# Last stage of a two-layer trunk: where the weight sums for four of eleven pairs of blocks are made

## The chip, the cores and the metric

The kernel runs on one core of a Trainium2 chip. The metric is device microseconds of one execution; the kernel before took 1689.75 us as the median of three runs (1689.26, 1689.75 and 1690.2). The engines are named as the profile names them: PE (matrix multiply; PEld is its weight load), DVE (vector), ACT (scalar), POOL (GpSimd) and SP, which only issues DMAs here. POOL and ACT issue DMAs too. Each engine takes its instructions in one fixed order and waits at the first one whose inputs or buffers are not ready.

## The reference, cut to what matters

Two residual layers, 512 positions, width 1024. Each layer has a token mixer with three branches, an output projection, and a gated feed-forward block with a causal convolution; a last RMSNorm follows. The change touches how the second layer's down projection gets its weights:

```python
def conv_ffn(h, w_up, conv_w, conv_b, w_down):
    u = h @ w_up                                  # 512 x 1024 by 1024 x 5632
    ...
    gate, val = jnp.split(c, 2, axis=-1)          # 2 x 2816 columns
    return (jax.nn.silu(gate) * val) @ w_down     # 2816 x 1024
...
    x = x + conv_ffn(rmsnorm(x, norm2_g[l]), ffn_w_up[l], ffn_conv_w[l], ffn_conv_b[l], ffn_w_down[l])
return rmsnorm(x, final_g)
```

## The kernel before, in words

**Numbers.** Every fp32 product is made of three matmuls on parts: a value is split into hi (a rounded copy, made by ACT) and lo (the rest, made by DVE as value minus hi), and `mm3` (line 153) multiplies hi by lo, hi by hi and lo by hi. A weight block of 128 x 512 is a *unit*: `load` (line 122) fetches it over SP's queue into a raw buffer, `part` (line 131) splits it (ACT copy at line 140, DVE subtraction at line 141), and the matmuls at line 157 use it. `unit` (line 95) works ahead by a plan of all units known beforehand: for the last stage's units (pool "q") it splits up to 4 units ahead of the one in use (`AHEAD`) and loads up to 6 ahead of the splits (`DEEP`). Hi and lo of three units in five go to ring buffers of three (tiles wh and wl), of the other two to the general pool of 31 tiles, tag "u" (tiles sh and sl).

**The order of the program.** First layer: mixer, output projection, up projection `ffn_up` (22 steps), down projection `ffn_down` (line 1160, 8 steps). Second layer: mixer, output projection, `ffn_up`, and then `last` (line 1182), the second down projection with the final norm.

**The last stage.** The 2816 rows of the second layer's w_down are 22 blocks of 128; block pair q (0 to 10) has blocks 2q and 2q+1, each cut into two halves of 512 columns: four quarters, b[0] to b[3]. `last` multiplies by a scheme with seven products per pair in place of eight. Four of them, p = 7, 5, 6, 4, need sums of the quarters: 7 is b3 - b1, 5 is b1 - b0, 6 is b0 plus sum 7, and 4 is b2 minus sum 6. **The first phase** of `last` runs through the pairs with these four products (44 units, n = 4q for p = 7, then 5, 6, 4); each unit feeds six matmuls. The PSUM tiles of products 7 and 5 are named acc in the profile, those of 6 and 4 are named sm. Later phases use the plain quarters.

**Where the sums were made before.** `presum` (line 246) makes them ahead of time in the first layer: on a call it finishes the pair that is pending (four DVE sums at lines 251 to 254 and four stores to DRAM from POOL's queue at line 257, tiles ts) and starts the next one by the table `PRE` (four loads from POOL's queue at line 262, tiles pre). Pairs 0 to 3 are started in steps 2, 4, 6, 8 of the first `ffn_up`, pairs 4 to 10 one after each of the first seven steps of the first `ffn_down`. The first phase of `last` then loads the finished sums over SP's queue (wr<-ts) and splits them.

**Beside the splits** the first phase makes others: `side(n)` (line 1206) fetches stored activations over SP's queue, and splits one (`both`, lines 1200 to 1204: an ACT copy at 1202 and a DVE subtraction at 1203) after every fourth unit and another after every eighth. From pair 2 on (`self.keep = q > 1`) splits and these others stay in program order on their engines: copy and subtraction of unit n + 4, then those of `side(n)`, then those of unit n + 5.

At the start of the first phase DVE and ACT also finish the last step of `ffn_up`: the convolution (lines 1125 to 1132) and `halves` (lines 1144 to 1158), which takes one of the three wh buffers.

Of the kernel before, what the change touches and what calls it, by code (L numbers as in the profile page):

```python
# [13 lines left out]
ADD, SUB, MUL, POW, MAX = ALU.add, ALU.subtract, ALU.mult, ALU.pow, ALU.max  # L14
# [9 lines left out]
FIRST = (12, 4, 0, 8)  # L24
FILL = (36, 2, 1)
KEPT = 6
PRE = {(0, "f", 2): 0, (0, "f", 4): 1, (0, "f", 6): 2, (0, "f", 8): 3, (0, "d", 0): 4, (0, "d", 1): 5, (0, "d", 2): 6, (0, "d", 3): 7,
       (0, "d", 4): 8, (0, "d", 5): 9, (0, "d", 6): 10}
SEQ = "0 H G G 0 S 0 U U G G 0 S 0 0 S 2 2 Y 0 0 2 1 2 1 2 1 2 1 2 1 2 1 1 1"
NRAW = 3  # L30
AHEAD = {None: 2, "p": 4, "r": 3, "f": 3, "u": 5, "q": 4}
# [21 lines left out]
class Emit:  # L53
# [67 lines left out]

    def load(self, u, queue=None):
        name, l, i, c0, n, _ = u
        raw = self.u(n="wr") if u[5] in ("q", "u") and self.nraw % 2 else self.wp.tile([128, 512], F32, name=self.nm("wr"), tag="wr", bufs=NRAW)
        src = self.tsum[i] if name == "tsum" else self.a[name][l, i]
        with self.tc.high_priority():
            self.kept((queue or self.nc.sync).dma_start(raw[:, :n], src[:, c0:c0 + n]))
        self.raws.append(raw)
        self.nraw += 1

    def part(self, u):
        raw, n, pool = self.raws.pop(0), u[4], u[5]

        self.turn = (self.turn + 1) % 5 if pool in ("p", "q") else 4
        if pool is None or self.turn < 3:
            hi, lo = [self.wp.tile([128, 512], F32R, name=self.nm(t), tag=t, bufs=3) for t in ("wh", "wl")]
        else:
            hi, lo = [{"f": self.f, "r": self.r, "u": self.u, "p": self.u, "q": self.u}[pool](dt=F32R, n=t) for t in ("sh", "sl")]
        with self.tc.high_priority() if pool in (None, "p", "q") else nullcontext():
            self.kept(self.nc.scalar.copy(hi[:, :n], raw[:, :n]))  # L140
            self.kept(self.nc.vector.tensor_tensor(lo[:, :n], raw[:, :n], hi[:, :n], op=SUB))  # L141
        self.parts.append((hi, lo))
        self.npart += 1
# [102 lines left out]
    def presum(self, l, stage, m):  # L246

        if self.pre:
# [6 lines left out]
            for p, t in zip((7, 5, 6, 4), (b[3], b[1], b[0], b[2])):  # L255
                self.tsum[q, p] = self.dp.tile([128, 512], F32, name=self.nm("ts"))
                self.nc.gpsimd.dma_start(self.tsum[q, p], t)
        q = PRE.get((l, stage, m))
        if q is not None:
# [89 lines left out]
    def run(self):  # L349
        nc, tc, a, V = self.nc, self.tc, self.a, self.nc.vector  # L350
        self.con = self.cp.tile([128, NCC], F32, name="con")
        self.pre, self.tsum = [], {}
        self.rst = self.cp.tile([128, 512], F32, name="rst")
        self.bonesR = self.cp.tile([128, 128], F32R, name="bonesR")
        self.ones = self.cp.tile([128, 128], F32R, name="ones")
        V.memset(self.rst, 1.0)
        wu = self.acc()
        for i in range(5):
            nc.tensor.matmul(wu[:, 0:256], self.rst[:, 0:128], self.rst[:, 256:512], start=True, stop=True)  # L359
        st = self.norm_new()  # L360
        first = tc.tile_pool(name="x0", bufs=1)
        x0 = first.__enter__().tile([128, 520], F32, name="x0g", tag="x0g")
        self.pc = x0[:, 512:520]
        xs = [x0[:, 0:512]] + [self.u(n="x") for _ in range(7)]
        self.keep = True
        with tc.high_priority():
            for j in range(8):
                q, o, i = (nc.scalar, xs[j], a["xT"][:, j, :]) if j in (1, 3) else (nc.sync, xs[j], a["xT"][:, j, :])
                tc.keep_in_program_order(q.dma_start(*((o, i) if j else (x0, a["x0g"]))))
                if self.plan and j in (0, 1, 2):  # L370
                    self.load(self.plan[self.nraw], nc.sync if j else nc.scalar)
        tc.keep_in_program_order(nc.scalar.copy(self.small((128, 1), "ms"), self.rst[:, 0:1]))
        tc.keep_in_program_order(nc.scalar.copy(self.ones, self.rst[:, 0:128]))
        for step in "z0 w z1 w z2 w z3 s0 s1 w z4 s2 z5 s3 w c z6 s4 w z7 s5 s6 s7 w w".split():
            if step == "w":
                if self.plan:
                    if self.nraw == self.npart:
                        self.load(self.plan[self.nraw])
                    self.part(self.plan[self.npart])
            elif step == "c":  # L380
                g1 = self.pc
                self.load_pc(0)
                tc.keep_in_program_order(nc.scalar.dma_start(self.con, a["con"]))
                self.pc, g1 = g1, self.pc
            elif step[0] == "z":
                self.norm_z(st, xs[int(step[1])], "n1")
            else:
                self.norm_sq(st, xs[int(step[1])])
        self.keep, self.pc = False, g1
        first.__exit__(None, None, None)  # L390
        xd = [a["xT"][:, j, :] for j in range(8)]
        for l in range(L):
            mg = self.mixer(l, st)
            st = self.norm_new()
            x = self.wout(l, mg, xd, st)
            st["sq"] = self.split(st["acc"])
            act = self.ffn_up(l, st, x if l == L - 1 else None)
            if l == L - 1:
                self.last(act)
            else:  # L400
                st = self.norm_new()
                x, xd = self.ffn_down(l, act, x, st)
                st["sq"] = self.split(st["acc"])
            self.rp.__exit__(None, None, None)
            self.fp = None
# [771 lines left out]
    def last(self, act):  # L1177
# [7 lines left out]

        def unit(p, q):
            if p > 3:
                return self.unit("tsum", 0, (q, p), 0)
            return self.unit("wdt", 0, 2 * q + (p > 1), 512 * (p == 3))

        def prod(ps, x, at, r, w, first, end, **kw):
# [56 lines left out]
        for q in range(Q):  # L1248
            self.keep = q > 1
            s, t = act[q][:2]  # L1250
            for p in (7, 5, 6, 4) if q < Q - 1 else (6, 7, 5, 4):
                w = unit(p, q)
                side(n)
                n += 1
                x, at = {7: (t, 0), 5: (s, 0), 6: (s, 256), 4: (t, 256)}[p]
                for r in range(2):
                    prod(pss[p][r], x, at, r, w, q == 0, q == Q - 1)
                if q == Q - 1 and p in (6, 7):
                    for r in range(2):
                        (e1 if p == 6 else f0).append(half(pss[p][r]))  # L1260
            if q == 1:
                for h in range(2):
                    nc.gpsimd.dma_start(fg[h], self.a["fgr"][:, H[h]].to_broadcast([128, 512]))
# [17 lines left out]
        for q in range(Q):  # L1281
            w = unit(1, q)
            if q == 0:
                ab.append(both(*raws.pop(0)))
            elif q == 2:
                ab.append(both(*raws.pop(0)))
            elif q == 4:
                s4.append(both(*raws.pop(0)))
            for r in range(2):
                go(1, q, r, w)  # L1290
            if q < 2:
                v[2, q], v[3, q] = addx(pss[5][q], 1, 2 + q), addx(pss[5][q], 1, q)
            elif q < 4:
                v[1, q - 2] = addx(pss[4][q - 2], 0, q)
            elif q < 6:
                y, r = e1[q - 4], q - 4
                for j in range(4):
                    c = lambda t: t[:, 128 * j:128 * j + 128].rearrange("p (a d) -> p a d", d=32)
                    V.tensor_tensor(c(y), self.xt[j][:, r], c(y), op=SUB)
                v[0, r] = y  # L1300
# [27 lines left out]
        for q in range(Q):  # L1328
            w = unit(2, q)
            for r in range(2):  # L1330
                go(2, q, r, w)
            post(q)
        for q in range(Q - KEPT):
# [7 lines left out]
            elif q < 4:  # L1341
                y, b = v[0, q - 2], ss[:, q - 2:q - 1]
# [7 lines left out]
        for r in range(2):  # L1350
            y, ya, b = v[3, r], v[0, r], bias[:, r:r + 1]
# [130 lines left out]
```

## Time and profile before

| what | value |
|---|---|
| median of three runs | 1689.75 us (1689.26 to 1690.2) |
| span of the profiled execution, first to last instruction | 1688.8 us |
| the median less that span | 0.95 us |
| granted TensorE clock over the span | 1.000 |
| DVE busy over the span | 1217.9 us |
| ACT busy over the span | 793.7 us |
| POOL busy over the span | 261.3 us |
| moved by DMA | 260.01 MB |

The profile is one execution. Its views give spans in microseconds from the first instruction; a time of the profiled execution outside its span is not given, so the median of the runs stands 0.95 us above the span. In a timeline row the first number is the start, the second the duration, "x2" two instructions merged, and the brackets hold the idle time of the engine ahead of the row and what ended it. In the chain of waits a row is start, duration, and the instructions that the end of the kernel hung on in that time.

### The profile page before, as it was taken

The page shows a single profiled execution, that of the slowest core. Times are in us where ns is not written, and L with a number is a line of the kernel's source. Part 1 is how long each engine was busy: PE and PEld are TensorE (multiplying, and loading weights), DVE is VectorE, ACT ScalarE, POOL GpSimd, SP SyncE. Part 2 cuts the span into 40 slices and gives each one's busy share as a digit, 9 for nine tenths or more (in the row PEclk, how much of TensorE's full clock was granted, in tenths as well). Part 3 has the DMA queues.
Part 4 walks back from the last instruction along what each step waited for, and adds up shares of the span by engine and source line. Part 5 has one row for each costly group of instructions (what it writes and reads, how often), then busy time and mean ns, then how long its engine had stood idle before and what let it go on. Part 6 is the DMA issues. An engine that isn't in the chain of part 4 may idle for free.

```text
span 1688.8 us, 27952 instructions
## 1 busy us (share of the span) xinstructions
PE 1680.2 (99%) x10247; PEld 1381.5 (82%) x10247; DVE 1217.9 (72%) x2115; ACT 793.7 (47%) x1365; POOL 261.3 (15%) x376
## 2 busy tenths in 40 slices
PE   9999999999999999999999999999999999999998
PEld 7888877888888888888888888778888888888887
DVE  7887746578669877655568888465786688887877
ACT  6563433554255444433346544335542544444565
POOL 1121000312301200003321210003122012220000
PEclk9999999999999999999999999999999999999999
DMA  5236563634544533247743366536344434443775
GB/s 183 88 109 199 176 187 95 184 122 134 191 144 148 195 122 97 63 146 261 252 145 99 94 207 184 174 101 188 118 137 163 154 96 144 142 141 110 244 248 177
DMA packets 143385, 260.01 MB, mean 154 GB/s; under 512 B 19440, under 2 KB 35440, under 8 KB 143248
## 3 DMA queue, kind: packets, MB, share of 16 engines
q1 hardware_dynamic: 117056, 188.41, 35.9%
q0 software_dynamic: 17552, 54.15, 9.8%
q10 hardware_dynamic: 8640, 15.67, 2.6%
q8 instruction: 80, 1.31, 0.3%
q14 instruction: 57, 0.47, 0.1%
HBM read 212.94 MB, written 45.22 MB: 153 GB/s over the span
## 4 chain that ended last, share of the span: by engine, by line
PE 97%; DVE 1%; DMA 1%; issue 0%; ACT 0%; SPq 0%; ACTq 0%; DVEq 0%
PE acc L157 88%; PE sm L157 3%; PE sm L696 2%; PE sm L948 1%; PE sm L603 1%; PE sm L1059 0%; DMA wr<-wall 0%; DMA tr<-bkT 0%; DVE wl L141 0%; PE acc L359 0%; PE sm L566 0%; PE sm L565 0%; PE sm L1006 0%; PE sm L850 0%; PE acc L319 0%
## 5 line engine op out<-in xcount | busy, mean ns | idle before, releaser
L157 PE MATMUL acc<-lo,sh 128*128 128x512 f32 x1108 | 432.0, 390 | 0.0
L157 PE MATMUL acc<-hi,sh 128*128 128x512 f32 x1108 | 431.4, 389 | 0.0
L157 PE MATMUL acc<-hi,sl 128*128 128x512 f32 x1108 | 424.6, 389 | 0.0
L140 ACT CAST sh<-wr 128x512 fp32r<-128x512 f32 (+1 forms) x375 | 226.8, 614 | 309.1 <-PE acc L157 165.6
L141 DVE TENSOR_TENSOR sl<-wr,sh 128x512 fp32r<-128x512 f32 (+1 forms) x375 | 252.0, 680 | 94.9 <-ACT sh L140 78.9
L141 DVE TENSOR_TENSOR wl<-wr,wh 128x512 fp32r<-128x512 f32 x238 | 169.0, 713 | 139.4 <-ACT wh L140 133.6
L140 ACT CAST wh<-wr 128x512 fp32r<-128x512 f32 x238 | 146.8, 619 | 242.8 <-PE acc L157 154.6
L157 PEld LDWEIGHTS acc<-lo,sh 128*128 128x128 f32 x1108 | 208.0, 188 | 43.8 <-issue 0.3
L157 PEld LDWEIGHTS acc<-hi,sl 128*128 128x128 f32 x1108 | 208.0, 188 | 43.1 <-issue 0.2
L157 PEld LDWEIGHTS acc<-hi,sh 128*128 128x128 f32 x1108 | 208.0, 188 | 43.0
L157 PE MATMUL acc<-lo,wh 128*128 128x512 f32 x584 | 230.0, 394 | 0.4 <-DVE rwp L525 0.4
L157 PE MATMUL acc<-hi,wl 128*128 128x512 f32 x584 | 228.3, 391 | 0.1
L157 PE MATMUL acc<-hi,wh 128*128 128x512 f32 x584 | 227.6, 390 | 0.0
L1125 ACT ACTIVATE cv<-fu,pc 128x512 f32<-128x512 f32 x88 | 71.7, 816 | 138.4 <-DVE fu L1123 138.4
L157 PEld LDWEIGHTS acc<-hi,wl 128*128 128x128 f32 x584 | 109.6, 188 | 24.6 <-issue 0.9
L157 PEld LDWEIGHTS acc<-lo,wh 128*128 128x128 f32 x584 | 109.6, 188 | 24.2 <-DVE rwp L525 0.8
L157 PEld LDWEIGHTS acc<-hi,wh 128*128 128x128 f32 x584 | 109.7, 188 | 22.3 <-issue 0.2
L157 PE MATMUL acc<-ah,sh 128*128 128x512 f32 x352 | 108.4, 389 | 0.0
L1126 DVE SCALAR_TENSOR_TENSOR cv<-fu,pc,cv 128x511 f32<-128x511 f32 x88 | 65.8, 749 | 34.5 <-ACT cv L1125 34.4
L157 PE MATMUL acc<-wl,hi 128*128 128x512 f32 x212 | 85.7, 404 | 0.0
L1123 DVE TENSOR_TENSOR fu<-acc,rsF 128x512 f32<-128x512 f32 x88 | 60.3, 685 | 30.8 <-PE acc L157 29.8
L157 PE MATMUL acc<-wh,hi 128*128 128x512 f32 x212 | 82.5, 389 | 0.0
(368 smaller groups left out, 2447.5 us busy)
## 6 DMA issues: line engine op xcount, KB each, us to landing
wr<-wall SPq DMA_DIRECT2D x480, 256.0 KB, 2.9
gd<-gth ACTq DMA_DIRECT2D x48, 256.0 KB, 3.4
gth<-gd POOLq DMA_DIRECT2D x48, 256.0 KB, 3.7
pre<-wdt POOLq DMA_DIRECT2D x44, 256.0 KB, 6.1
ts<-pre POOLq DMA_DIRECT2D x44, 256.0 KB, 2.8
wr<-ts SPq DMA_DIRECT2D x44, 256.0 KB, 4.1
wr<-wdn SPq DMA_DIRECT2D x40, 256.0 KB, 4.3
wr<-wdt SPq DMA_DIRECT2D x33, 256.0 KB, 4.1
```

The costliest lines, as they stand in the source:

```text
L140: self.kept(self.nc.scalar.copy(hi[:, :n], raw[:, :n]))
L141: self.kept(self.nc.vector.tensor_tensor(lo[:, :n], raw[:, :n], hi[:, :n], op=SUB))
L157: i = self.nc.tensor.matmul(*x, **y, **kw)
L603: i = T.matmul(pK[hv[1 - h], j, :], bk[hv[h], c, 1, :], x[hv[h], c, :], start=True, stop=True)
L696: po(T.matmul(o, l, r, start=start, stop=True, skip_group_check=True))
L948: po(T.matmul(o, lhsT, rhs, start=start, stop=stop, skip_group_check=True))
L1123: V.tensor_tensor(u, ps, self.rsF, op=MUL)
L1125: A.activation(t, u, AF.Identity, scale=self.p("cw2", j), bias=self.p("cb", j))
L1126: V.scalar_tensor_tensor(t[:, 1:], u[:, :511], self.p("cw1", j), t[:, 1:], op0=MUL, op1=ADD)
```

## The change

Pairs 2, 4, 6 and 8 (`NOW`) are taken out of `PRE`. The table now starts pairs 0, 1, 3, 5 in steps 2, 4, 6, 8 of the first `ffn_up`, and pairs 7, 9, 10 after steps 0, 2, 4 of the first `ffn_down`. For the four pairs in `NOW`, units of the first phase are named "tnow": when the first of a pair's four comes up to be loaded, `fetch4` loads all four plain quarters over SP's queue (b1, b3, b0, b2) into four tiles of the "u" pool named now; when a unit comes up to be split, `sum4` makes its sum on DVE in place, and ACT and DVE split the result. Order is kept where the splits' order is kept.

```diff
-PRE = {(0, "f", 2): 0, (0, "f", 4): 1, (0, "f", 6): 2, (0, "f", 8): 3, (0, "d", 0): 4, (0, "d", 1): 5, (0, "d", 2): 6, (0, "d", 3): 7,
-       (0, "d", 4): 8, (0, "d", 5): 9, (0, "d", 6): 10}
+NOW = (2, 4, 6, 8)
+PRE = {(0, "f", 2): 0, (0, "f", 4): 1, (0, "f", 6): 3, (0, "f", 8): 5, (0, "d", 0): 7, (0, "d", 2): 9, (0, "d", 4): 10}
...
     def load(self, u, queue=None):
         name, l, i, c0, n, _ = u
+        if name == "tnow":
+            self.raws.append(i)
+            self.nraw += 1
+            if i[1] == 7 or i[0] not in self.now:
+                self.fetch4(i[0], queue)
+            return
...
+    def fetch4(self, q, queue):
+
+        b = self.now[q] = [self.u(n="now") for _ in range(4)]
+        with self.tc.high_priority():
+            for i in (1, 3, 0, 2):
+                self.kept((queue or self.nc.sync).dma_start(b[i], self.a["wdt"][0, 2 * q + i // 2][:, i % 2 * 512:i % 2 * 512 + 512]))
+
+    def sum4(self, q, p):
+
+        b = self.now[q]
+        o, i, op = {7: (3, 1, SUB), 5: (1, 0, SUB), 6: (0, 3, ADD), 4: (2, 0, SUB)}[p]
+        with self.tc.high_priority():
+            self.kept(self.nc.vector.tensor_tensor(b[o], b[o], b[i], op=op))
+        return b[o]
+
     def part(self, u):
         raw, n, pool = self.raws.pop(0), u[4], u[5]
+        if type(raw) is tuple:
+            raw = self.sum4(*raw)
...
             if p > 3:
-                return self.unit("tsum", 0, (q, p), 0)
+                return self.unit("tnow" if q in NOW else "tsum", 0, (q, p), 0)
```

More of the change, by code (lines that the diff above doesn't have):

```diff
@@ L351, in run @@
         self.con = self.cp.tile([128, NCC], F32, name="con")
-        self.pre, self.tsum = [], {}
+        self.pre, self.tsum, self.now = [], {}, {}
         self.rst = self.cp.tile([128, 512], F32, name="rst")
```

## The prediction, made before the changed kernel ran

> **What bounds the kernel now.** I read the page first, then the chain of waits in order of time, then tables by stretch of the two places that the change touches, and last the timelines of single engines.
>
> ```profile
> span 1688.8 us, 27952 instructions
> PE 1680.2 (99%) x10247; PEld 1381.5 (82%) x10247; DVE 1217.9 (72%) x2115; ACT 793.7 (47%) x1365; POOL 261.3 (15%) x376
> PE 97%; DVE 1%; DMA 1%; issue 0%; ACT 0%; SPq 0%; ACTq 0%; DVEq 0%
> ```
>
> PE is the bound: 97% of the chain that ended last is PE, and it is idle for 1688.8 - 1680.2 = 8.6 us in all. Work that is moved on another engine matters only where PE would wait for it. So the question is whether PE waits where the work leaves (the first down projection) or where it arrives (the first phase of the last stage).
>
> The next rows are the chain of waits around both places.
>
> ```profile
> 505.97 355.19 PE acc L157 x1567
> ...
> 1599.35 2.72 PE acc L157 x12
> ...
> 1612.95 2.72 PE sm L157 x12
> ...
> 1618.39 2.72 PE sm L157 x12
> ```
>
> From 505.97 to 861.16 us, most of the first up projection and all of the first down projection, the chain is one unbroken run of 1567 matmuls, 355.19 / 1567 = 0.2267 us apart. In the last stage twelve matmuls, two units, take 2.72 us: again 0.2267 us each, so a unit is 1.36 us of PE. The table by stretch (length, then busy time and count of each engine, clock, DMA share, GB/s) shows the same:
>
> ```profile
> core 0: us, PE busy (x) PEld busy (x) DVE busy (x) ACT busy (x) POOL busy (x), PEclk, DMA share, GB/s
> 680.00:740.00 60.00, 60.00 (x267) 49.67 (x266) 41.28 (x62) 25.55 (x41) 0.00 (x0) 1.00 0.23 70
> 740.00:800.00 60.00, 60.00 (x266) 49.69 (x265) 31.66 (x55) 19.67 (x34) 17.14 (x32) 1.00 0.73 238
> 800.00:860.00 60.00, 60.00 (x266) 49.69 (x265) 32.75 (x51) 18.25 (x31) 17.17 (x32) 1.00 0.74 247
> 1591.00:1635.00 44.00, 44.00 (x195) 36.41 (x194) 31.12 (x55) 28.21 (x51) 0.00 (x0) 1.00 0.90 300
> ```
>
> 740 to 860 is the first down projection. PE does as many matmuls there as in the 60 us before it, at three times the DMA share. DVE is half idle. In the first phase of the last stage (1591 to 1635) PE is full too, and DVE is busy 31.1 of 44 us.
>
> **What is removed.** The operations of `presum` are these:
>
> ```profile
> L262 POOL DMA_DIRECT2D pre<-wdt x44: 536/538/543, 451.5 to 841.6; - x44
> L257 POOL DMA_DIRECT2D ts<-pre x44: 539/543/553, 534.3 to 852.3; - x44
> L251 DVE TENSOR_TENSOR pre<-pre,pre x11: 684/692/694, 533.3 to 849.1; 128x512 f32<-128x512 f32 x11
> ```
>
> Four pairs leave the first down projection: 16 sums x 0.69 = 11 us of DVE, 16 loads and 16 stores x 0.54 = 17 us of POOL's issuing, 32 x 256 KB = 8.4 MB of DMA. PE's run there has no gap, so this is worth **0 us**. The steps of the up projection have as many pairs as before, only other ones: 0 us.
>
> **What is added.** SP loads 16 plain quarters in place of 16 sums. Over the stretch 1540 to 1640 us the two cost the same:
>
> ```profile
> wr<-ts SPq DMA_DIRECT2D x44, 256.0 KB, 4.1
> wr<-wdt SPq DMA_DIRECT2D x10, 256.0 KB, 4.1
> ```
>
> Bytes and queue stay. The second to fourth load of a pair move up past what SP would have issued between them, a stored activation at most, and four tiles are held at once. I take 0 us, because these loads are asked for ten units ahead of their use (6 + 4), 13.6 us of PE against 4.1 us to land; without that cover a late load is a stall of PE, priced below.
>
> The price is the 16 sums on DVE, and more than their own time. The order on DVE is kept: sum(n), subtraction(n), sum(n + 1). The subtraction waits for ACT's copy, the copy for the sum. So the next sum stands in the queue behind a subtraction that waits. From rows of DVE and ACT:
>
> ```profile
> 1582.23 0.42 DVE L1154 TENSOR_TENSOR wh<-wh,fth 128x256 f32<-128x256 f32 x1
> 1602.77 0.69 DVE L141 TENSOR_TENSOR wl<-wr,wh 128x512 fp32r<-128x512 f32 x1 [0.67 <-ACT wh L140]
> 1603.38 0.69 DVE L1203 TENSOR_TENSOR lo<-sp,hi 128x512 fp32r<-128x512 f32 x1
> 1606.85 0.69 DVE L141 TENSOR_TENSOR wl<-wr,wh 128x512 fp32r<-128x512 f32 x1 [0.79 <-ACT wh L140]
> ...
> 1582.69 0.62 ACT L149 CAST ah<-wh 128x512 fp32r<-128x512 f32 x1 [0.60 <-DVE wh L1154]
> 1606.19 0.62 ACT L140 CAST wh<-wr 128x512 fp32r<-128x512 f32 x1 [0.93 <-PE acc L157]
> ```
>
> A sum takes 0.69 us; ACT starts 0.04 us after DVE ends (1582.65 to 1582.69); DVE starts 0.66 us after ACT started (1606.19 to 1606.85); and the next DVE instruction starts 0.61 us after (1602.77 to 1603.38). One unit with its sum thus takes 0.69 + 0.04 + 0.66 + 0.61 = **2.00 us of DVE's queue, against 1.36 us of PE**. A unit without takes 0.61, and so does each `both`. Eight units, one pair with sums and one without, have three `both`: 4 x 2.00 + 7 x 0.61 = 12.27 us against 8 x 1.36 = 10.88 us. DVE's queue becomes the bound of such a period by **1.4 us**, once the lead of the splits over PE is used up.
>
> The Trainium skill, "VectorE: DVE Perf Modes", section "The DRAIN you can't avoid", says that the next vector operation does not start until the pipe of the one before is empty. Taken as end of one row to start of the next, that would be 0.69 for each 0.61, and 2.3 us a period. The rows above start 0.61 us apart while each lasts 0.69, so the trace's pace stands.
>
> **How much lead there is.**
>
> ```profile
> 1585.73 0.43 DVE L1157 TENSOR_TENSOR fth<-fth 128x256 f32<-128x256 f32 x1 [0.81 <-DMA ab<-fth]
> 1588.48 0.68 DVE L141 TENSOR_TENSOR sl<-wr,sh 128x512 fp32r<-128x512 f32 x1
> 1592.23 0.69 DVE L141 TENSOR_TENSOR wl<-wr,wh 128x512 fp32r<-128x512 f32 x1 [2.47 <-ACT wh L140]
> 1596.25 1.30 DVE L141 TENSOR_TENSOR wl<-wr,wh 128x512 fp32r<-128x512 f32 x2 [0.77 <-ACT wh L140]
> 1613.65 0.69 DVE L141 TENSOR_TENSOR wl<-wr,wh 128x512 fp32r<-128x512 f32 x1 [1.58 <-ACT wh L140]
> ...
> 1586.81 0.19 PEld L157 LDWEIGHTS sm<-wl,ah 128*128 128x128 f32 x1 [0.38 <-DVE wl L141]
> ...
> 1589.67 0.39 PE L157 MATMUL acc<-sl,ah 128*128 128x512 f32 x1
> ...
> 1599.19 0.39 PE L157 MATMUL acc<-wl,ah 128*128 128x512 f32 x1
> ```
>
> Counting units from PE's rows (n = 8 is pair 2's first, n = 16 pair 4's): unit 9 is ready at 1588.48 + 0.68 = 1589.16 and used at 1589.67, lead 0.5. Unit 7 has none: PE's weight load waits 0.38 us for it. Unit 16 is the second of the two at 1596.25, ready at 1597.55 and used at 1599.19: lead 1.6. Full lead is reached later: unit 30 is ready at 1613.65 + 0.69 = 1614.34 and used at 1618.39, lead 4.05; more there cannot be, since its wh buffer comes free when PE ends unit 25 at 1612.95.
>
> **The sum.** From a pair's first unit with a sum to its fourth DVE needs 3 x 2.00 + 0.61 (one `both`) = 6.61 us, PE 3 x 1.36 = 4.08: a lead of 2.53 is eaten. From a fourth unit without lead to the first of the next such pair DVE needs 7 x 0.61 + 0.69 + 0.04 + 0.66 = 5.66, PE 5 x 1.36 = 6.80: 1.14 is won back.
> - Pair 2 (order not kept): four sums x 0.61 = 2.4 us in a stretch of DVE that has idle times of 0.81 and 2.47 us. They can fit, or delay units 7 to 9, which have 0 to 0.5 us of lead: 0 to 2.4 us. A stall here hands the same time to unit 16 as lead, so with pair 4 it counts once; I take 0, nearest to the idle rows.
> - Pair 4: 2.53 - 1.6 = 0.9 us (bounds 0 with full lead, 2.5 with none).
> - Pairs 6 and 8: 2.53 - 1.14 = 1.4 us each. With full lead at unit 16, pair 6 loses nothing and pair 8 1.3.
> - Pairs 9 and 10 win lead back; the tail shifts as a whole.
>
> 0.9 + 1.4 + 1.4 = **3.7 us**: span 1692.5. The median stood 0.95 above the span, so 1693.4 us; bounds 1.3 and 2.4 + 0.9 + 2.8 = 6.1 us.
>
> **The rivals.** A measurement of this kernel tells about 0.2% from no change, 3.4 us: the border to slower is 1693.1.
> - *The lead is enough* (the other side: not slower). In plain work, eight units are 15 x 0.61 = 9.2 us of DVE, under PE's 10.88. If the loads of quarters, freed from the raw buffers, land earlier and unit 16 starts with 4 us of lead, or if sums get ahead of waiting subtractions, PE loses 0 to 1.7 us: 1689.7 to 1691.5. It decides from 3.0 us of lead at unit 16. For it: full lead at unit 30. Against it: 0.5 to 1.6 us in units 9 to 16.
> - *Pair 2's sums on the path, or quarters late.* The sums go ahead of `halves`, which holds the wh buffer that unit 7 waits for; or SP waits for four free tiles at once. Section one costs 2.4 us, later pairs no less than above: +5 to +6.1, 1694.8 to 1696. For it: the wait of 0.38 us, and a DMA share of 0.90. Against it: those idle times of DVE.
> - *Matmuls in the first down projection speed up* when DMA there falls. Their 0.2267 us would have to be stretched by it; the 60 us at share 0.23 hold as many matmuls as those at 0.73. Saving 5% in 120 us would give 1683.7. The Trainium skill, "TensorE: Matmul & The Clock Gate", section "Back-to-back issue gap", has 512 / 2.4 + 2.5 = 216 ns for an isolated warm gap of this width, 5% under the rows; the equal counts say that DMA is not the reason.
> - *Another order elsewhere*: the rest of the program is arranged anew and PE's 8.6 idle us shrink or grow by a few.
>
> **How the numbers follow.** Forecast 1693.4 (own range 1692.4 to 1694.8): 0.48, of which 0.31 over the border. Enough lead: 0.25. On the path: 0.18. Faster matmuls: 0.02. Another order: 0.07, of which 0.05 faster. So faster 0.07, slower 0.31 + 0.18 + 0.01 = 0.50, within 0.2% 0.43. The range 1689.4 to 1696.0 leaves out the faster cases, the lowest part of "enough lead" and some of "on the path", 0.2 together.
>
> **What would show it.** In the profile after: 1567 matmuls in 355 us as before in the first down projection, with fewer POOL rows; in the first phase DVE rows of a sum, a subtraction 1.39 us later, the next sum 0.61 after that; PE waiting for DVE subtractions of units 18 and 19, 26 and 27, 34 and 35, about 0.6 us each, and in no unit of pairs 3, 5, 7. Wrong it would be if those subtractions are ready ahead of PE; if SP's or DMA's waits stand ahead of the sums; or if the first down projection gets shorter.

## The result, and the profile after

The changed kernel took 1699.19 us (median of four runs, 1698.37 to 1700.13), the kernel before beside it 1689.97 us (four runs, 1689.26 to 1690.47): a ratio of 1.0051, 95% interval 1.004 to 1.0063. It is slower by half a per cent, about 9 us, and lies above the whole forecast range. The profiled run took 1699.79 us. In the new file the lines below the edit stand 23 further down: the matmul of `mm3` is L180, the split's copy L163 and subtraction L164, the sum L149, the quarters' load L142, the convolution L1146 to L1150, and `halves` L1174 to L1180.

From the page of the kernel after: the span, the busy engines, and the share of each in the chain that ended last.

```profile
span 1697.8 us, 27883 instructions
PE 1683.8 (99%) x10247; PEld 1383.4 (81%) x10247; DVE 1215.6 (72%) x2115; ACT 793.9 (47%) x1365; POOL 243.1 (14%) x344
PE 93%; issue 4%; DVE 1%; DMA 1%; ACT 0%; POOL 0%; DVEq 0%; POOLq 0%; ACTq 0%
```

The span grew by 9.0 us. PE has the same 10247 matmuls, is busy 3.6 us longer, and idle 1697.8 - 1683.8 = 14.0 us in place of 8.6. So something made matmuls wait, and something made matmuls slow.

The next rows are a table by stretch of the kernel after: busy time and count of each engine, granted clock, DMA share, GB/s.

```profile
core 0: us, PE busy (x) PEld busy (x) DVE busy (x) ACT busy (x) POOL busy (x), PEclk, DMA share, GB/s
1583.70:1587.40 3.70, 0.47 (x3) 0.04 (x1) 3.63 (x9) 0.62 (x1) 1.96 (x4) 1.00 0.85 268
1587.40:1591.80 4.40, 4.38 (x12) 3.34 (x12) 1.17 (x2) 1.24 (x2) 0.20 (x1) 0.62 0.95 319
740.00:800.00 60.00, 60.00 (x266) 49.72 (x265) 29.12 (x50) 19.88 (x34) 10.74 (x20) 1.00 0.63 197
800.00:860.00 60.00, 60.00 (x267) 49.69 (x266) 25.22 (x40) 18.35 (x32) 6.44 (x12) 1.00 0.47 149
```

The first down projection (740 to 860) lost POOL, DVE and DMA work, and PE did 533 matmuls in 120 us where it had done 532: nothing came back. The loss is in the last stage. From 1583.7 PE stands still for most of 3.7 us, and in the next 4.4 us it does 12 matmuls where the clock is 0.62.

The chain of waits of the kernel after has the same two anchors as the one shown of before, and one more behind pair 8; below it is the last anchor of the kernel before.

```profile
505.80 355.19 PE acc L180 x1567
...
1605.80 2.72 PE acc L180 x12
...
1638.17 4.08 PE sm L180 x18
```

```profile
1629.27 4.08 PE sm L157 x18
```

The first down projection's run of 1567 matmuls lasts 355.19 us in both. Unit 16 (pair 4's first) is 1605.80 - 1599.35 = 6.45 us later than before, and the row behind pair 8 is 1638.17 - 1629.27 = 8.90 later; no wait of PE follows up to the end of the phase. Nearly three quarters of the loss was made in or just before pair 2, before any sum of pair 4 was used.

PE in that place, first after, then before (start, duration; brackets: idle time and what ended it):

```profile
1583.55 0.62 PE L180 MATMUL acc<-sh,ah 128*128 128x512 f32 x2
1587.42 0.79 PE L180 MATMUL acc<-wl,ah 128*128 128x512 f32 x1 [3.25 <-DVE wl L164]
...
1591.13 0.39 PE L180 MATMUL sm<-wl,ah 128*128 128x512 f32 x1
...
1593.22 0.50 PE L180 MATMUL sm<-wl,ah 128*128 128x512 f32 x1 [1.25 <-DVE wl L164]
```

```profile
1583.95 0.39 PE L157 MATMUL acc<-wl,ah 128*128 128x512 f32 x1
...
1586.81 0.50 PE L157 MATMUL sm<-wl,ah 128*128 128x512 f32 x1
```

The first row that waits is unit 5: 1587.42 in place of 1583.95, 3.47 us late. The nine matmuls from there (unit 5's six and three of unit 6) take until 1591.13, 3.71 us in place of 9 x 0.2267 = 2.04: 1.67 us more, in the stretch with the clock at 0.62. Then unit 7 waits 1.25 us more, and starts at 1593.22 in place of 1586.81: 6.41 us late. These are units of pair 1, whose sums were made long before. What they wait for is DVE:

```profile
1579.16 1.42 DVE L149 TENSOR_TENSOR now<-now,now 128x512 f32<-128x512 f32 x2 [1.26 <-DMA now<-wdt]
...
1581.15 0.68 DVE L149 TENSOR_TENSOR now<-now,now 128x512 f32<-128x512 f32 x1
...
1583.02 0.68 DVE L149 TENSOR_TENSOR now<-now,now 128x512 f32<-128x512 f32 x1
1583.62 0.68 DVE L164 TENSOR_TENSOR sl<-now,sh 128x512 fp32r<-128x512 f32 x1
1584.22 0.68 DVE L1155 SCALAR_TENSOR_TENSOR fth<-fth,cv 128x512 f32<-128x512 f32 x1
1584.83 0.68 DVE L164 TENSOR_TENSOR sl<-now,sh 128x512 fp32r<-128x512 f32 x1
...
1586.68 1.28 DVE L164 TENSOR_TENSOR wl<-wr,wh 128x512 fp32r<-128x512 f32 x2
...
1592.14 0.42 DVE L1180 TENSOR_TENSOR fth<-fth 128x256 f32<-128x256 f32 x1 [3.58 <-DMA ab<-fth]
1592.48 0.68 DVE L164 TENSOR_TENSOR wl<-wr,wh 128x512 fp32r<-128x512 f32 x1
```

```profile
1578.92 0.75 DVE L1126 SCALAR_TENSOR_TENSOR cv<-fu,pc,cv 128x511 f32<-128x511 f32 x1 [0.89 <-ACT cv L1125]
...
1580.98 0.68 DVE L1132 SCALAR_TENSOR_TENSOR fth<-fth,cv 128x512 f32<-128x512 f32 x1
...
1583.03 1.28 DVE L141 TENSOR_TENSOR wl<-wr,wh 128x512 fp32r<-128x512 f32 x2
```

The first fence is DVE's order after, the second three rows of before. All four sums of pair 2 and two of its subtractions (1583.62 and 1584.83, units 8 and 9) now stand in the middle of `ffn_up`'s last convolution, ahead of the splits of units 5 and 6 (the two at 1586.68, before at 1583.03: 3.65 us later). The sums are 4 x 0.61, the two subtractions 2 x 0.60: together 3.6 us. DVE's idle 0.89 us there, before for ACT, is taken by a wait of 1.26 for the quarters: SP issued them from 1573.57 on, and the sums stand so far ahead that DVE was ready for them 4.3 us later.

Unit 7's split hangs on something else. It stands behind L1180, which overwrites half of an activation tile that is being stored (ab). DVE waited 3.58 us there for that store. POOL issues it when the activation (fth) is ready:

```profile
1585.20 0.54 POOL L1175 DMA_DIRECT2D ab<-fth  x1 [13.24 <-DVE fth L1155]
```

```profile
1581.96 0.54 POOL L1152 DMA_DIRECT2D ab<-fth  x1 [9.86 <-DVE fth L1132]
```

So the store went out 3.24 us later. And it took longer: the overwrite began 1592.14 - 1585.20 = 6.94 us behind the issue, before 1585.73 - 1581.96 = 3.77. In the ten microseconds around it (first 1583 to 1593 after, then 1579 to 1589 before) more was on the way:

```profile
DMA packets 1423, 2.92 MB, mean 292 GB/s; under 512 B 171, under 2 KB 171, under 8 KB 1422
...
now<-wdt SPq DMA_DIRECT2D x4, 256.0 KB, 6.1
```

```profile
DMA packets 849, 1.81 MB, mean 181 GB/s; under 512 B 117, under 2 KB 117, under 8 KB 848
```

The four quarters of pair 4 are among it. The step was late by 3.24 + 3.17 = 6.41 us, just what unit 7 was late. The slow matmuls lie in the shadow of this wait: without them PE would have stood at unit 7 for that much longer.

In pair 4 the pattern on DVE is the one forecast:

```profile
1603.00 0.68 DVE L149 TENSOR_TENSOR now<-now,now 128x512 f32<-128x512 f32 x1
1604.45 0.69 DVE L164 TENSOR_TENSOR wl<-now,wh 128x512 fp32r<-128x512 f32 x1 [0.76 <-ACT wh L163]
1605.06 0.69 DVE L149 TENSOR_TENSOR now<-now,now 128x512 f32<-128x512 f32 x1
...
1607.04 0.68 DVE L149 TENSOR_TENSOR now<-now,now 128x512 f32<-128x512 f32 x1
```

From sum to sum 2.06 and 1.98 us, against PE's 1.36. PE's waits in pairs 6 and 8 follow; the last row is of before:

```profile
1621.52 0.50 PE L180 MATMUL sm<-wl,ah 128*128 128x512 f32 x1 [0.39 <-DVE wl L164]
...
1625.74 0.39 PE L180 MATMUL sm<-wl,ah 128*128 128x512 f32 x1
...
1631.76 0.50 PE L180 MATMUL sm<-sl,ah 128*128 128x512 f32 x1 [0.33 <-DVE sl L164]
...
1633.81 0.50 PE L180 MATMUL sm<-wl,ah 128*128 128x512 f32 x1 [0.39 <-DVE wl L164]
```

```profile
1618.23 0.39 PE L157 MATMUL sm<-wl,ah 128*128 128x512 f32 x1
```

Unit 30, behind pair 6, is at 1625.74, before 1618.23: 7.51 late, so pair 6 cost 1.06. Another 1.39 came with pair 8. The account is 6.45 + 1.06 + 1.39 = 8.90 us.

### The profile page after: what moved, and what is told of

It reads as the page before. It is cut to its first block, busy times and chain, and to the rows that moved or that the text cites. A ratio compares the mean times of both kernels' runs of the same rounds, so it can differ in the third digit from the quotient of the medians.

```text
span 1697.8 us, 27883 instructions
## 1 busy us (share of the span) xinstructions
PE 1683.8 (99%) x10247; PEld 1383.4 (81%) x10247; DVE 1215.6 (72%) x2115; ACT 793.9 (47%) x1365; POOL 243.1 (14%) x344
## 4 chain that ended last, share of the span: by engine, by line
PE 93%; issue 4%; DVE 1%; DMA 1%; ACT 0%; POOL 0%; DVEq 0%; POOLq 0%; ACTq 0%
PE acc L180 84%; PE sm L180 3%; PE sm L719 2%; PE sm L971 1%; PE sm L626 1%; PE sm L1082 0%; DMA ab<-fth 0%; DMA wua<-wua 0%; DVE wl L164 0%; PE acc L382 0%; ACT wh L163 0%; PE sm L589 0%; PE sm L588 0%; PE sm L1029 0%; DVE sl L164 0%
## 5 line engine op out<-in xcount | busy, mean ns | idle before, releaser
L180 PE MATMUL acc<-lo,sh 128*128 128x512 f32 x1108 | 432.0, 390 | 0.0
L180 PE MATMUL acc<-hi,sh 128*128 128x512 f32 x1108 | 431.4, 389 | 0.0
L180 PE MATMUL acc<-hi,sl 128*128 128x512 f32 x1108 | 424.6, 389 | 0.0
L163 ACT CAST sh<-wr 128x512 fp32r<-128x512 f32 (+1 forms) x368 | 222.4, 614 | 297.4 <-PE acc L180 187.2
L164 DVE TENSOR_TENSOR sl<-wr,sh 128x512 fp32r<-128x512 f32 (+1 forms) x368 | 247.4, 680 | 111.7 <-ACT sh L163 74.2
L164 DVE TENSOR_TENSOR wl<-wr,wh 128x512 fp32r<-128x512 f32 x229 | 161.2, 707 | 128.8 <-ACT wh L163 125.9
L163 ACT CAST wh<-wr 128x512 fp32r<-128x512 f32 x229 | 141.3, 619 | 228.5 <-PE acc L180 163.5
L180 PEld LDWEIGHTS acc<-hi,sl 128*128 128x128 f32 x1108 | 208.0, 188 | 43.6 <-issue 0.2
L180 PEld LDWEIGHTS acc<-lo,sh 128*128 128x128 f32 x1108 | 208.1, 188 | 43.5 <-issue 0.3
L180 PEld LDWEIGHTS acc<-hi,sh 128*128 128x128 f32 x1108 | 208.1, 188 | 42.7
L180 PE MATMUL acc<-lo,wh 128*128 128x512 f32 x584 | 230.0, 394 | 0.3 <-DVE rwp L548 0.3
L180 PE MATMUL acc<-hi,wl 128*128 128x512 f32 x584 | 228.0, 390 | 0.0
L180 PE MATMUL acc<-hi,wh 128*128 128x512 f32 x584 | 227.6, 390 | 0.0
L180 PEld LDWEIGHTS acc<-lo,wh 128*128 128x128 f32 x584 | 109.6, 188 | 23.9 <-DVE rwp L548 0.7
L180 PEld LDWEIGHTS acc<-hi,wl 128*128 128x128 f32 x584 | 109.6, 188 | 23.8 <-issue 0.9
L180 PEld LDWEIGHTS acc<-hi,wh 128*128 128x128 f32 x584 | 109.7, 188 | 22.4 <-issue 0.2
L180 PE MATMUL acc<-ah,sh 128*128 128x512 f32 x352 | 108.4, 389 | 0.0
L180 PE MATMUL acc<-wl,hi 128*128 128x512 f32 x212 | 85.8, 405 | 0.0
L1146 DVE TENSOR_TENSOR fu<-acc,rsF 128x512 f32<-128x512 f32 x88 | 60.3, 685 | 32.4 <-PE acc L180 31.3
L180 PE MATMUL acc<-wh,lo 128*128 128x512 f32 x212 | 82.5, 389 | 0.0
```

The lines of the kernel that those rows point to most:

```text
L180: i = self.nc.tensor.matmul(*x, **y, **kw)
L1146: V.tensor_tensor(u, ps, self.rsF, op=MUL)
```

## The experiments

Each kernel is the changed one with one edit, timed beside the kernel before on the same chip. That one's median was 1690.58 us beside the runs of single pairs, of no sums and of the first with TensorE fed, 1690.27 beside those on the order of sums and on the gains' loads, and 1690.26 beside the others. A cost in us is the median less that one.

**Which pairs cost what.** Two kernels part the change.

```diff
-NOW = (2, 4, 6, 8)
+NOW = (4, 6, 8)
```

(pair 2 is made in the first layer again, with the seven that the change left there).

> Pair 2 goes back to the first layer; pairs 4, 6 and 8 keep their sums in the last stage. Theory (pair 2's sums ahead of the splits of units 5 to 7 cost some 6.7 us, pairs 4, 6 and 8 cost by DVE's queue alone): no wait above 1 us and no slow clock in the last stage, pair 4 loses 0.9 us (its lead is 1.6 us again), pairs 6 and 8 1.0 to 1.4 each, so 3 to 3.7 us over before, about 1693. Rival (the four loads at once, or the DMAs of the last stage, cost the time whatever the pair): 5 us or more over before, 1695 or later.

1695.26 us, ratio 1.0027 (1.0017 to 1.0037): 4.7 us. From DVE's and then from PE's timeline:

```profile
1597.02 0.69 DVE L164 TENSOR_TENSOR wl<-now,wh 128x512 fp32r<-128x512 f32 x1 [0.77 <-ACT wh L163]
```

```profile
1598.35 0.39 PE L180 MATMUL acc<-wl,ah 128*128 128x512 f32 x1
...
1604.39 0.50 PE L180 MATMUL sm<-sl,ah 128*128 128x512 f32 x1 [0.33 <-DVE sl L164]
```

Pair 4's first unit is ready at 1597.02 + 0.69 = 1597.71 and used at 1598.35: a lead of 0.6, not of the 1.6 that the prediction took from a plain unit. From there to the pair's fourth unit PE needs 6.04 us in place of 3 x 1.36 = 4.08: 2.0 us lost. The remaining 2.7 are pairs 6 and 8, forecast at 2.8: PE waits there at units 26, 27, 34 and 35. The other half, pair 2 alone:

```diff
-NOW = (2, 4, 6, 8)
+NOW = (2,)
```

> Only pair 2 has its sums in the last stage. Theory: the wait of unit 5, the slow matmuls after it and the wait of unit 7 stay, 6 to 7 us over before, 1696 to 1697, and no wait after unit 12. Rival (loss spread over all four pairs): about a quarter of 9.2 us, 1692.

1695.69 us, ratio 1.0031 (1.0019 to 1.0043): 5.1 us. From PE's timeline and the table by stretch:

```profile
1586.95 0.80 PE L180 MATMUL acc<-wl,ah 128*128 128x512 f32 x1 [3.30 <-DVE wl L164]
...
1590.56 0.39 PE L180 MATMUL sm<-wl,ah 128*128 128x512 f32 x1
```

```profile
1588.00:1592.00 4.00, 4.00 (x15) 3.20 (x14) 2.42 (x5) 2.31 (x4) 0.00 (x0) 0.74 0.42 134
```

Unit 5 waits as in the whole change (3.46 us from start to start), and the nine matmuls behind it take 3.61 us in place of 2.04, the mean clock from 1588 to 1592 being 0.74. No later unit waits. 3.46 + 1.57 = 5.0 of the 5.1. The halves, 4.7 and 5.1, add up to 9.8 against 8.6 to 9.2 for the whole (ratio and medians): nearly additive, so pair 2 is over half of it.

This run also parts the two things that made the store late. POOL's and DVE's rows:

```profile
1584.73 0.54 POOL L1175 DMA_DIRECT2D ab<-fth  x1 [8.29 <-DVE fth L1155]
```

```profile
1588.02 0.42 DVE L1180 TENSOR_TENSOR fth<-fth 128x256 f32<-128x256 f32 x1
```

The store goes out late here too, but no quarters of pair 4 are loaded beside it: it lands 2.7 us after its issue, DVE doesn't wait for it, and PE doesn't wait for unit 7. So the late issue alone doesn't stop unit 7. Over all runs of this document the store took 2.6 to 3.9 us in the five whose loads of pair 4's quarters don't start within 2 us of it (the kernel before among them), and 4.5 to 6.9 us in the nine where they do.

**The sums, or what comes with them.** The next kernel keeps loads and tiles and leaves the sixteen sums out (its products use plain quarters in their place).

```diff
-            raw = self.sum4(*raw)
+            raw = self.now[raw[0]][{7: 3, 5: 1, 6: 0, 4: 2}[raw[1]]]
```

> As after, but the 16 sums of the last stage are left out: the units of these four pairs split the plain quarters (the result of these products is another one). Loads, buffers and the emptier first down projection are as in after. Theory (the sums on DVE are the price, and the first down projection gives nothing back): 1689.5 to 1690.5, as before. Rival 1 (loads of four quarters at once): 1693 or later. Rival 2 (the first down projection gains): under 1688.5.

1691.79 us, ratio 1.0006 (0.9997 to 1.0015). So the loads from elsewhere, the four tiles held at once and the work taken from the first down projection come together to a loss of 1.2 us (by the interval, a gain of 0.5 to a loss of 2.5). Units 5 and 7 still wait about 0.8 us each there; the store of ab took 5.2 us. The rest of the 9 us needs the sums.

**The order in pairs 4, 6 and 8.** Here those three pairs alone have sums, and each sum is put on DVE ahead of the subtraction of the unit before it, so that no sum stands behind a subtraction that waits for ACT. The work is the same.

```diff
-            raw = self.sum4(*raw)
+            raw = self.ahead.pop(raw) if raw in self.ahead else self.sum4(*raw)
...
+            if self.raws and type(self.raws[0]) is tuple:
+                self.ahead[self.raws[0]] = self.sum4(*self.raws[0])
```

(the added lines stand between the copy and the subtraction in `part`).

> Pairs 4, 6 and 8 as in the run with these three, but each sum is put on DVE ahead of the subtraction of the unit before it, so that ACT's copy never waits for a sum that waits for a subtraction. Same instructions, another order. Theory (the turn of 2.00 us a unit is the loss of these pairs): a unit costs DVE 1.21 us, under PE's 1.36, so the 4.7 us of that run fall to 0 to 1: 1690.5 to 1691.5. Rival (DVE's busy time, or late loads): 1694 or later.

1690.53 us, ratio 1.0002 (0.9993 to 1.0010): the 4.7 us are gone. DVE's timeline in pair 6 (the subtraction is L166 in this file):

```profile
1609.23 0.68 DVE L149 TENSOR_TENSOR now<-now,now 128x512 f32<-128x512 f32 x1
1609.83 0.68 DVE L166 TENSOR_TENSOR wl<-now,wh 128x512 fp32r<-128x512 f32 x1
1610.43 0.68 DVE L149 TENSOR_TENSOR now<-now,now 128x512 f32<-128x512 f32 x1
```

A unit with its sum takes 1.20 us of DVE in place of 2.00, since ACT's copy of one unit runs beside DVE's work on the other. That is under PE's 1.36. It was the place of the sum in the queue, not its 0.69 us.

**Order kept from pair 1 on.** Splits and sums of pair 2 then stay behind those of pair 1.

```diff
-            self.keep = q > 1
+            self.keep = q > 0
```

> As after, but program order is kept from pair 1 on, so pair 2's sums and splits stand on DVE behind the splits of units 5, 6 and 7 and behind the feed-forward's last instructions. Theory (the order of pair 2 made the long waits): no wait over 2 us and no slow clock; instead pair 2 pays 2.00 us a unit like the others, some 2.5 us, and pairs 4, 6 and 8 1.3 to 2 each, so 5.5 to 7 us over before, about 1697, and 2 to 3 under after. Rival (the loads of quarters alone make the waits): the waits of units 5 and 7 stay at 3 and 1.4 us and the time at 1699.

1699.36 us, ratio 1.0052 (1.0039 to 1.0065): no gain, against expectation. Unit 5 no longer waits, but unit 7 does (DVE's timeline):

```profile
1587.34 0.42 DVE L1180 TENSOR_TENSOR fth<-fth 128x256 f32<-128x256 f32 x1 [3.07 <-DMA ab<-fth]
```

The store was issued at 1581.32, as early as before, but the overwriting could begin only 6.0 us later: beside the quarters the store took 5.9 us. And pair 2, now with DVE's turn of 2.00 us and no lead, lost about 2.5 us of its own. One cost went, another came in its place.

**All four pairs with the sums ahead, order kept from pair 1.** Both edits together.

> All four pairs, order kept from pair 1 on, and each sum ahead of the subtraction before it. Theory: pairs 4, 6 and 8 lose nothing, pair 2 delays unit 7 by one sum (0.6 us) and then keeps up: 0.5 to 2.5 us over before, 1691 to 1693. Rival (the work of four pairs does not fit in the first phase in any order): 1695 or later.

1692.90 us, ratio 1.0015 (1.0006 to 1.0024): 2.6 us are left of about 9. In the profile unit 7 waits, for 1.0 us, since DVE's overwriting waits 1.66 us for the store. That profile is of the run with 1691.02 us, the lowest of eleven (up to 1694.72), so what makes up the rest of the 2.6 isn't shown.

**TensorE fed.** Does the slow clock come from the wait, and does it cost? Twelve matmuls of a zero weight tile are put between units 4 and 5, in the whole change and in the kernel with pair 2 alone.

```diff
+                if (q, p) == (1, 5):
+                    for _ in range(12):
+                        po(nc.tensor.matmul(pss[7][0], zero, act[0][0][0], start=False, stop=False))
```

> As after, with 12 matmuls of a weight of zeros added into the PSUM tile of product 7 between units 4 and 5, where PE waits 3.4 us (2.7 us of PE work; one small DVE instruction makes the zeros). Theory (a wait as long as this one drops the granted clock, and the ten matmuls behind it take 0.43 us in place of 0.23): the clock stays at 1.00 and the time falls by 1.5 to 2 us against after, to about 1697.4, though PE does more. Rival (the slow matmuls come from DMA or from memory ports): no change or slower, 1699 or later.

1701.27 us, ratio 1.0058 (1.0046 to 1.0071): not the gain that was expected. Unit 4 then waits 1.08 us and unit 5 0.55, and no matmul behind them is slow. But unit 7 still hangs on the store, now for longer, and the slow clock came there (PE's timeline, and the table for this stretch and for the one ahead of it):

```profile
1593.49 0.79 PE L180 MATMUL sm<-wl,ah 128*128 128x512 f32 x1 [2.42 <-DVE wl L164]
```

```profile
1593.40:1596.60 3.20, 3.10 (x7) 2.48 (x8) 1.93 (x4) 0.75 (x3) 0.00 (x0) 0.50 0.70 271
1584.00:1593.00 9.00, 6.52 (x28) 4.73 (x26) 5.71 (x12) 1.89 (x4) 2.16 (x4) 1.00 0.90 295
```

The time is what the rival forecast, the trace is not: at a DMA share of 0.90 the clock was 1.00 as long as TensorE was fed, and at 0.70 it was 0.50 behind the wait. So the load on DMA doesn't make the slow matmuls here.

> Sums in pair 2 alone, and between units 4 and 5 TensorE gets twelve matmuls of a zero weight tile (added to an accumulator, the result is not changed), so that it is never without work for 3 us. Theory (the granted clock falls because TensorE stood still for 3.46 us in one piece, and in the run with pair 2 alone the slow matmuls behind it are on the path): the same work is late by the same time, but no matmul runs at 0.43 us and the mean clock of 1584 to 1592 is 0.95 or more; 1.2 to 1.6 less than that run, 1694.1 to 1694.5. Rival (the clock falls for another reason, or its matmuls are hidden): no less than 1695.3, and matmuls at 0.43 us still.

With pair 2 alone, where nothing waits for the store: 1693.92 us, ratio 1.0021 (1.0012 to 1.0030), against 1.0031 without the fed matmuls. The mean clock from 1584 to 1592 is 1.00, and no matmul is slow. The intervals overlap; by the costs of the two (5.1 and 3.7) the slow clock cost 1.4 us there, by the two profiled spans (1693.2 and 1692.3) 0.9. So it seems to cost where nothing else is late in its shadow; in the whole change unit 7's wait covered it.

**The gains' loads behind the store.** The two loads of the norm's gains (fg) stand ahead of the second store on POOL; they are moved behind it.

```diff
-            if q == 1:
+            if q == 7:
```

> As after, but the two loads of the final norm's gains are issued from POOL's queue behind the feed-forward's last stores and not ahead of them. Theory (the wait of unit 7 hangs on the store that took 6.85 us, beside these loads and four loads of quarters): the store lands 1 to 3 us sooner, unit 7 waits less, and the ten slow matmuls become the longer path: 0.7 to 1.5 us under after, 1697.7 to 1698.5. Rival (SP's loads of quarters alone delay the store): the same as after.

1700.10 us, ratio 1.0058 (1.0046 to 1.0071): no gain. The overwriting began 6.0 us behind the store's issue in place of 6.9, and still waited 2.62. These loads are a small part of what lengthens the store.

**A tile of its own.** In the last pair a0 - a1 goes to a tile that nobody stores, so no DVE instruction waits for the ab store.

```diff
+        if q == NFF // 2 - 1:
+            o = self.own
+            self.nc.scalar.copy(o[:, h[1]], b[:, h[1]])
+            V.tensor_tensor(o[:, h[0]], a[:, h[0]], a[:, h[1]], op=SUB)
+            b = o
```

> As the changed kernel, but a0-a1 of the last pair goes to a tile of its own (ScalarE copies the other half there), so that no instruction on VectorE waits for the ab store. Theory (unit 7 is late by the store that halves waits for; unit 5 by the order): the wait of 3.58 us in front of that subtraction and TensorE's 1.41 us at unit 7 go; unit 5's 3.4 and the slow matmuls behind it stay; pair 4, which loses the lead that the stall at unit 7 gave it, may take up to 1 back: 1697.6 to 1698.6. Rival (unit 7 is late by the order of VectorE's queue alone, the store only ends last): as the changed kernel, 1699 or more.

1698.20 us, ratio 1.0048 (1.0035 to 1.0061), as expected, but by its interval no different from the change itself. The trace, of the run with 1699.60 us, says more than the time: unit 7 does not wait, unit 5 waits as before, and the clock from 1588 to 1592 is 0.62. The slow matmuls, hidden in the change, are on the path here.

> As the run before with a tile of its own for a0-a1, and twelve matmuls of a zero weight tile between units 4 and 5 as well. Theory (three things cost in pair 2: the order, the store, and behind the store's wait the slow clock, each hiding the next): unit 4 and 5 late by 1.2 and 0.7 and twelve matmuls of 0.23, that is 4.7 in place of 3.4 and 1.7 of slow matmuls, no wait at unit 7, no matmul at 0.43 us: 1696.2 to 1697.6. Rival (the store's wait is covered by something else that comes as late): 1699 or more.

With the fed matmuls as well: 1700.36 us, ratio 1.0055 (1.0043 to 1.0068), against expectation. Units 5 and 7 came as forecast and the clock stayed at 1.00. But PE lost 1.0 us in pair 4 now, which the larger stall had covered, and some 1.6 us at 1646 to 1651, where units of a later phase wait for DVE. Why they wait there isn't shown. Nor does the trace explain the time: the profiled spans are 1697.0 here and 1697.6 without the fed matmuls, while the medians lie 2.2 us apart the other way.

> All four pairs with each sum put ahead of the subtraction of the unit before it, the order kept from pair 1 on, and the tile of its own for a0-a1. Theory (order and store are all that the change costs): the wait of 1.04 us at unit 7 goes too, 1690.2 to 1691.4. Rival (the sixteen sums or their loads cost something by themselves): 1692 to 1693, as without the tile.

All four pairs with sums ahead, order kept and the tile of its own: 1691.29 us, ratio 1.0007 (0.9998 to 1.0016). The time is in the range expected, the reason isn't shown: in the profile, of the run with 1692.62 us, PE still waits 1.0 us, at unit 5 now, since DVE stood 1.29 us for the quarters ahead of pair 2's first sum; and the interval overlaps that of the kernel without the tile. No kernel here was faster than the one before.

## Why the prediction was wrong, step by step

- *PE is the bound, and the first down projection gives nothing back*: right. 1567 matmuls in 355.19 us in both, and without the sums the change gains nothing. The rival of faster matmuls is out.
- *The loads cost nothing*: right in size (1.2 us without the sums), wrong in one respect: beside pair 4's quarters the store of ab takes 4.5 to 6.9 us in place of 3.7, and DVE waits for it. The ten units of cover were counted up to PE's use; the sums of pair 2 were put far ahead of that, and DVE waited 1.26 us for their quarters.
- *A unit with its sum takes 2.00 us of DVE*: right, 1.98 to 2.06, with the next sum 0.61 us behind the subtraction. The Trainium skill's rule in "VectorE: DVE Perf Modes", section "The DRAIN you can't avoid", taken as end to start, would have made a turn longer; the rows after again start 0.60 apart at a length of 0.68.
- *Pairs 6 and 8, 1.4 us each*: 1.06 and 1.39 after, 2.7 together in the kernel without pair 2, with PE's waits at units 26, 27, 34 and 35 and none in pairs 3, 5 and 7. Right in mechanism and size. That the place of the sum makes it is shown by the kernel with the sums ahead.
- *Pair 4, 0.9 us*: with pair 2 as before it was 2.0, because the lead was 0.6; in the change it was 0, because pair 2's stall handed DVE the lead. The prediction had said that the two count once together, but it charged pair 4 and left pair 2 at nothing; it was the other way round. (The full lead of 4.05 at unit 30 is 3.9: PE's timeline has that unit at 1618.23, while 1618.39 is the chain's row. No term rests on the difference.)
- *Pair 2, 0 us*: **this is the step that failed.** It took "four sums x 0.61 = 2.4 us in a stretch of DVE that has idle times of 0.81 and 2.47 us" and chose 0 as "nearest to the idle rows". Those idle times lie at 1585.73 and 1592.23, behind the splits of units 5 and 6. The sums were put ahead of them, into the convolution, where DVE had only 0.89 us of idle time (and it went to waiting for the quarters), and two subtractions of pair 2 went with them. In place of 0 to 2.4 us it cost 6.4: 3.5 at unit 5, and to unit 7 another 2.9, through a store that was issued 3.24 us later and took 3.17 longer. Of the 2.9 us, 1.7 are slow matmuls behind the first wait; without the store's wait they stay, as the kernel with a tile of its own shows. The prediction had read the wait of 0.81 us for that store in the same row, as room for sums; it was a wait that would grow.
- *The rival "pair 2's sums on the path, or quarters late"* had the place and the first cause, sums ahead of `halves`; it didn't have the store or the clock. It was given 0.18 at 2.4 us for the section. The upper bound of 6.1 us rested on that price, and so the range was too low. Pairs 6 and 8 it had at what they cost. The rival *the lead is enough* named, with sums that get ahead of waiting subtractions, what the kernel with the sums ahead then showed: next to no loss.

What made the sums go ahead is the arrangement of the program where the order isn't kept (pair 1's units): the sums are marked urgent there, and two subtractions went with them (why these two came ahead of units 5 and 6 isn't shown). Keeping the order from pair 1 took away unit 5's wait, which shows that the order made it; unit 7 waited there all the same, for a store issued on time that took 5.9 us beside the quarters, which shows the second cause.

## What to carry to other kernels

Before work is put "into idle time" of an in-order queue, find the place in the queue where it will stand, and count only the idle time ahead of the first instruction that somebody waits for. An idle time that ends in a DMA is no room but a wait; here it grew from 0.81 to 3.58 us when the store got company. An instruction that feeds another engine and gets its answer back belongs one turn ahead in the queue: that alone was 4.7 us here, for the same work.

## What was not expected of the hardware

After TensorE had stood still for 3.25 us the granted clock was 0.62 over the next 4.4 us: matmuls started 0.43 us apart in place of 0.23, for about 3.2 us. In the kernel with the gains' loads moved, the six matmuls behind a wait of 3.26 us still ran at full pace, and the slow ones began 1.5 us after the wait. The same slow pace followed a wait of 2.42 us (clock 0.50), but not one of 2.28 us at the same unit in the kernel with the order kept from pair 1, nor the 1.25 us of the change. The Trainium skill, "TensorE: Matmul & The Clock Gate", section "What's actually happening", has a clock halved after an idle window of about 3.4 us in a window that runs freely. Half speed, and the length of the slow stretch, agree; the 3.25 us come close to a whole window, the 2.42 us do not, so here a shorter wait was enough, at least in one run. In the kernel with pair 2 alone it cost some 0.9 to 1.4 us, where nothing else was late.
